# A hybrid decoder layer on one core: the gates' unit in two passes, rows of maxima laid by DMA, seam fills on another queue

## The chip, the cores and the metric

One core of a Trainium2 chip runs the whole layer in one launch. The metric is the device time of one execution in microseconds; the number given for a kernel is the median of three runs. A further execution was profiled, and all rows shown come from it.

## The reference

One layer, 2048 tokens of width 1024, float32. `proj = rmsnorm(x) @ w_in` feeds two groups of heads:

```python
q_ml, k_ml, v_ml, o_ml, gates        # mLSTM: 4 heads, chunkwise recurrence, gates = 8 columns of proj
c_q, c_kv, k_r = ...                 # MLA: 8 heads
q  = [rmsnorm(c_q) @ w_uq]           # 64 plain + 32 rotary columns a head
kv = [rmsnorm(c_kv) @ w_ukv]         # 64 key + 64 value columns a head
k  = concat(kv[..., :64], apply_rope(k_r, cos, sin))   # one rotary part (32) for all heads
p  = softmax(causal(q k^T / sqrt(96)));  h_mla = p v
x  = x + rmsnorm(concat(h_ml, h_mla) @ w_out)
x  = x + rmsnorm(relu(rmsnorm(x) @ w_up)^2 @ w_down)
```

The softmax needs the largest score of each query, or something near it, before `exp`.

## The kernel before

**Numbers.** Every float32 operand is split into a high part of type fp32r and the rest, and a product is three passes, high times high, high times rest, rest times high (`mm3`, L252 to 255: one line for each pass). The weights are split on the chip: ScalarE casts the high part (L464, L494), VectorE or GpSimd subtracts for the rest (L499). The rests are written to HBM (`wparts`) and loaded again for the later blocks of tokens (`wload`, L445), while the high part is made anew from the raw weights.

**Stages.** First come the input projections and the mLSTM, in four blocks of 512 tokens (0 to about 511 us). A block runs units of 128 columns, 8 k-tiles by 3 passes each: units 13 to 15 the latents, unit 0 a mixed one, 1 to 4 convolved q and k, 5 to 8 v, 9 to 12 the output gates, 16 to 18 the products behind the latents. The mixed unit 0 holds 8 gate columns, 56 of zeros, the 32 rotary key columns, and these again with their halves swapped. `stabiliser` (L962) scales its result into the tile `G`; `rotate` (L924) turns rows 64 to 95 with a table of sines in `trigd` and stores the turned keys in HBM (`krd`, L958 and L959).

Then comes attention (about 511 to 980 us): 8 heads by 4 query blocks of 512, called (h, qb). For each (h, qb) stand three kinds of work on TensorE: *maxima* `m` (L1594), which multiply high parts alone; scores `S` (L253 to 255, 3 passes); and products `o<-ph,V`, `o<-pl,V` and `o<-ph,onecol` (L1681, L1684, L1679). VectorE reduces each `m` to one column of `mp` (L1601, L1603), then all of a block to `mx`, 128 rows by 4 (L1622). To subtract a maximum from the scores, the operands have a 97th row: `K` has 1 there, `Q` the negative maximum. That row must lie along one partition, so TensorE turns `mx` by four matmuls with one column of weights each against the identity (`mt`, L1627), and ScalarE copies the 512 numbers, negated, from PSUM into row 96 of `QK` (L1630). The scores of (h, qb) wait for it. ScalarE takes two exponentials, VectorE or GpSimd subtracts them (`pl`, L1668). At the end of a (h, qb), `out_rows` (L1744) empties two accumulators: ScalarE copies 64 rows (`ot`, L1751), VectorE adds 64 (L1754) and copies the second accumulator (`ou`, L1758), GpSimd adds (L1761), and SP stores. The output projection and the MLP follow, to 2407 us; the change does not touch them.

**The seam.** At the end of the projections SBUF is handed over to attention in steps (`switch1` to `switch3`). Row 96 of `QK0` and `QK1` is filled from the input `edge` by three DMAs each, which GpSimd issues (`pool.dma_start`, L1496 and L1498); the fills of `V1` and `onecol` (L1492 to L1494) stand behind those of `QK1`. In the planner these six DMAs are put down as work of SP. SP issues all other loads: `krd` (L1540), `qkd` and `qrd` (L1546, L1548), values (L1561).

**What sets the order.** A planner (`Plan`, L130) gets every operation with its engine, a guessed duration, what it waits for, the buffers it takes and a key, runs them through in a time of its own, and writes each engine's instructions in the order found. Engines run that order strictly, each instruction waiting in place; SP does so with its DMAs too. GpSimd is POOL in the rows, VectorE DVE, ScalarE ACT, TensorE PE.

Of the kernel before, what the change touches and what calls it, by code (L numbers as in the profile page):

```python
# [10 lines left out]
F32 = mybir.dt.float32  # L11
# [43 lines left out]
OB = 1  # L55
QLO = 0
# [35 lines left out]
RB = (0, 0)  # L92
RK = (7, 7)
# [151 lines left out]
def trunk(ctx: ExitStack, tc: tile.TileContext, x, xT, pos, wu, wout, wup, wdn, cols, rows, consts, edge, out, dbg=None):  # L245
# [45 lines left out]
    qrd = dram.tile([2, P, 2, SEQ], F32, tag="qrd", name="qrd")  # L291
    krd = dram.tile([32, 2, SEQ], F32, tag="krd", name="krd")
# [24 lines left out]
    for name, bufs in (  # L317
        ("awr", WR), ("wh", 5), ("wl", 5), ("mma", 1), ("mmb", 1), ("pst", 1), ("chh", 1), ("sg", SG), ("cbc", 1), ("G", GB_), ("raw", 2), ("cy", 2), ("cth", 2),
# [27 lines left out]
    mrow = b1.tile([1, 20], F32, tag="mrow", name="mrow")  # L346
    cst8 = [b1.tile([P, 129], F32, tag=f"C{p}", name=f"C{p}") for p in range(2)]
# [39 lines left out]
    o_rest = pl.op("SP", 1000, load_rest, [o_fill], key=kA(0, 16), kb=70)  # L387

# [8 lines left out]
    o_fill2 = pl.op("Pool", 900, fills2, key=kA(0, -40))  # L397
    pl.op("Activation", 600, masks, [o_rest], key=kA(1, 0))
# [46 lines left out]
    def wload(b, u):  # L445
# [10 lines left out]
        def place_l():  # L456
            t["l"] = wp.tile([P, 1024], F32R, tag="wl", name=f"wl{b}_{u}", bufs=5)
# [14 lines left out]
        o_turn[:] = [gl]  # L472
# [4 lines left out]

    def wsplit(b, u):
        if b > STB[u]:
            return wload(b, u)  # L480
# [56 lines left out]
    def unit(b, u):  # L537
# [386 lines left out]
    def rotate(b, t, G):  # L924
# [4 lines left out]
        def load():  # L929
            t["tgr"] = e2.tile([P, TB], F32R, tag="cth", name=f"tg{b}")  # L930
            t["tg"] = f32(t["tgr"])
            dma(t["tg"][64:128], trigd[:, b * TB : (b + 1) * TB])
# [18 lines left out]
        g = pl.op("SP", 500, load, [o_rope[b % 2], G], key, take=("cth",), kb=128)  # L951
        o = pl.op(*cost, d1, [g, G], key)
# [9 lines left out]
    def stabiliser(b):  # L962
# [118 lines left out]
        h = pl.op("PE", 330, gates, [G, o_cst], key, take=("pst",), free=[("G", G)])  # L1081
# [1684 lines left out]
```

## Time and profile before

| | us |
|---|---|
| median of 3 runs | 2410.01 (2403.1 to 2412.87) |
| the profiled execution | 2408.7 |
| its span, first to last instruction | 2406.9 |
| TensorE busy, in the span | 2360.4 |
| VectorE, ScalarE, GpSimd busy | 1732.2, 1361.8, 815.3 |

How to read a row of a timeline: start in us, duration, engine, line, operation, what it writes and reads, count, and in brackets the idle time of its engine before it and what ended that. Successive matmuls overlap, so that a matmul's duration is longer than the step from its start to the next one's. DMA-issuing rows of SP and POOL show the issuing alone, not the transfer.

### The profile page before, as it was taken

The page shows a single profiled execution, that of the slowest core. Times are in us where ns is not written, and L with a number is a line of the kernel's source. Part 1 is how long each engine was busy: PE and PEld are TensorE (multiplying, and loading weights), DVE is VectorE, ACT ScalarE, POOL GpSimd, SP SyncE. Part 2 cuts the span into 40 slices and gives each one's busy share as a digit, 9 for nine tenths or more (in the row PEclk, how much of TensorE's full clock was granted, in tenths as well). Part 3 has the DMA queues.
Part 4 walks back from the last instruction along what each step waited for, and adds up shares of the span by engine and source line. Part 5 has one row for each costly group of instructions (what it writes and reads, how often), then busy time and mean ns, then how long its engine had stood idle before and what let it go on. Part 6 is the DMA issues. An engine that isn't in the chain of part 4 may idle for free. (4 is left out here: it accounts for less than half of the span.)

```text
span 2406.9 us, 34273 instructions
## 1 busy us (share of the span) xinstructions
PE 2360.4 (98%) x11141; PEld 1904.2 (79%) x11141; DVE 1732.2 (72%) x3105; ACT 1361.8 (57%) x2644; POOL 815.3 (34%) x698
## 2 busy tenths in 40 slices
PE   9999999989999999999999999999999999999997
PEld 7777878767777777788788888888888888888885
DVE  6867665658888888647767677766675677776777
ACT  5646454437778877444666556655564344433454
POOL 2725242538788888422000000000000223222346
PEclk9999999999999999999999999999999999999998
DMA  8697979886222321567777797665674445445358
GB/s 288 217 336 248 351 249 335 267 197 152 54 56 54 81 57 32 160 225 249 243 214 221 226 310 221 203 171 167 191 218 139 147 135 181 124 149 164 127 140 164
DMA packets 341308, 449.22 MB, mean 187 GB/s; under 512 B 34908, under 2 KB 227432, under 8 KB 341128
## 3 DMA queue, kind: packets, MB, share of 16 engines
q1 hardware_dynamic: 337192, 440.16, 58.7%
q0 software_dynamic: 3936, 6.87, 2.0%
q8 instruction: 88, 1.44, 0.3%
q14 instruction: 92, 0.75, 0.1%
HBM read 295.97 MB, written 153.05 MB: 187 GB/s over the span
## 5 line engine op out<-in xcount | busy, mean ns | idle before, releaser
L2575 POOL TENSOR_TENSOR y<-vd_0X,y 128x512 f32<-128x512 f32 x7 | 10.6, 1519 | 726.5 <-ACT vd_0X L2572 726.5
L1660 ACT ACTIVATE ph<-S 128x512 fp32r<-128x512 f32 (+1 forms) x320 | 170.3, 532 | 86.7 <-PE S L255 49.9
L1695 POOL TENSOR_TENSOR t<-t,ph 128x512 f32<-128x512 f32 (+1 forms) x192 | 212.9, 1109 | 17.3 <-ACT ph L1660 6.8
L2487 ACT CAST hh<-hr 128x512 fp32r<-128x512 f32 (+1 forms) x208 | 116.2, 567 | 157.0 <-PE d_5X L2538 15.4
L1668 DVE TENSOR_TENSOR pl<-S,ph 128x512 fp32r<-128x512 f32 (+3 forms) x271 | 156.4, 589 | 31.8 <-ACT S L1664 28.9
L253 PE MATMUL mm<-xh,wh 128*128 128x512 f32 x384 | 156.5, 408 | 4.2 <-DVE gate L1185 2.2
L2492 DVE TENSOR_TENSOR hl<-hr,hh 128x512 fp32r<-128x512 f32 (+1 forms) x208 | 133.0, 646 | 30.0 <-ACT hh L2487 23.5
L1601 DVE TENSOR_REDUCE mp<-m 128x1 f32<-128x512 f32 (+2 forms) x208 | 135.7, 666 | 25.2 <-PE m L1594 20.7
L254 PE MATMUL mm<-xl,wh 128*128 128x512 f32 x384 | 150.4, 392 | 0.8 <-DVE xl L424 0.8
L255 PE MATMUL mm<-xh,wl 128*128 128x512 f32 x384 | 150.3, 392 | 0.5 <-DVE wl L499 0.5
L1664 ACT ACTIVATE S<-S 128x512 f32<-128x512 f32 (+3 forms) x271 | 140.2, 517 | 0.4
L253 PE MATMUL S<-QK 97*128 97x512 f32 (+1 forms) x320 | 120.5, 377 | 2.1 <-DVE pl L1668 1.9
L1681 PE MATMUL o<-ph,V 128*128 128x512 f32 (+1 forms) x320 | 119.0, 378 | 1.8 <-DVE ot L1754 1.5
L1684 PE MATMUL o<-pl,V 128*65 128x512 f32 (+1 forms) x320 | 116.0, 363 | 3.4 <-POOL pl L1668 3.4
L1594 PE MATMUL m<-QK 96*128 96x512 f32 (+3 forms) x320 | 115.6, 388 | 1.8 <-DVE mp L1601 1.1
L254 PE MATMUL S<-QK 97*128 97x512 f32 (+1 forms) x320 | 116.9, 365 | 0.0
L255 PE MATMUL S<-QK 97*128 97x512 f32 (+1 forms) x320 | 116.7, 365 | 0.0
L253 PE MATMUL op<-wo,hh 128*128 128x512 f32 x256 | 100.9, 394 | 1.4 <-DVE osm L1985 1.0
L255 PE MATMUL op<-wo,hl 128*128 128x512 f32 x256 | 99.8, 390 | 0.0
L254 PE MATMUL op<-wo,hh 128*128 128x512 f32 x256 | 99.7, 389 | 0.0
L2326 ACT ACTIVATE t<-t 128x512 f32<-128x512 f32 x96 | 60.7, 632 | 65.0 <-DVE t L2321 64.6
L253 PEld LDWEIGHTS mm<-xh,wh 128*128 128x128 f32 x384 | 72.1, 188 | 22.8 <-DVE gate L1185 3.3
(6451 smaller groups left out, 7483.4 us busy)
## 6 DMA issues: line engine op xcount, KB each, us to landing
hr<-hd SPq DMA_DIRECT2D x100, 448.0 KB
wr<-in_wu_dram SPq DMA_DIRECT2D x71, 512.0 KB
hd<-t SPq DMA_DIRECT2D x128, 256.0 KB
hd<-ts SPq DMA_DIRECT2D x96, 256.0 KB
wl<-wparts SPq DMA_DIRECT2D x45, 512.0 KB
QK<-qkd SPq DMA_DIRECT2D x32, 512.0 KB
xt<-in_x_dram SPq DMA_DIRECT2D x28, 512.0 KB
xf<-xd SPq DMA_DIRECT2D x40, 256.0 KB
```

The costliest lines, as they stand in the source:

```text
L253: pe.matmul(o, ah, bh, start=start, stop=False)
L254: pe.matmul(o, ah, bl, start=False, stop=False)
L255: pe.matmul(o, al, bh, start=False, stop=stop)
L1601: vec.tensor_reduce(mp["t"][:, j, kb : kb + 1], ps[:, :n], axis=AX.X, op=ALU.max)
L1660: act.activation(t["h"][:, :w], t["S"][:, :w], AF.Exp)
L1664: act.activation(t["p"][:, :w], t["S"][:, :w], AF.Exp)
L1668: (pool if by_pool else vec).tensor_tensor(t["l"][:, :w], t["p"][:, :w], f32(t["h"][:, :w]), ALU.subtract)
L1681: pe.matmul(o0, v[:, 0:128], t["h"][:, :w], start=start, stop=stop)
L1684: pe.matmul(o1, v[:, 64:129], t["l"][:, :w], start=start, stop=stop)
L1695: pool.tensor_tensor(to, to, hv, ALU.add)
L2487: act.copy(t["h", m][:, :w], t["r", m][:, :w])
L2492: vec.tensor_tensor(t["l", m][:, :w], t["r", m][:, :w], f32(t["h", m][:, :w]), ALU.subtract)
```

## The change

Six things are changed.

1. **Unit 0 in two passes** (`wboth`). The rests of the 8 gate columns and of the 32 rotary columns are put into columns of the same tile that held zeros and the swapped copy. High and rest of the weights are then one operand, and unit 0 takes two passes a k-tile. The gates' high and rest are summed by the four small matmuls that turn them (`both8`, 16 rows in place of 8). Block 0 makes the tile and stores it; blocks 1 to 3 load it, 512 KB, with no raw weights and no cast.
2. **The rotary chain** (`rotate`) becomes longer for that: ScalarE copies the rest's 32 rows, an add joins them, and two DMAs inside SBUF make the swapped copy; the load of the sines stands behind the add.
3. **Rows of maxima of heads 1 to 7**: VectorE turns `mx` in 32x32 blocks (`mr`), and four DMAs inside SBUF, issued by SP, lay the 512 numbers into row 96. No matmul, no PSUM bank and no ScalarE copy is left there. Head 0 stays as it was. `K` has -1 in row 96 and `Q` the maximum.
4. **The second accumulator of heads 1 to 7** is copied by ScalarE in place of VectorE.
5. **At the seam**, the edge rows come from a copy of `edge` in HBM by DMAs on SP; GpSimd keeps the memsets, and `onecol` is filled ahead of `V1`. The scores wait for the edge rows, the maxima do not. The mask is loaded later, the rotary keys of `QK0` block by block, and the loads of head 1 wait for a given score step of head 0 each.
6. **Planner**: the second half of the sines is made from block 1 on, `out_rows` stores earlier by key, a weight's place waits for the cast of the one before, and some guessed durations are larger.

```diff
-RB = (0, 0)
-RK = (7, 7)
+RB = (0, 1)
+RK = (7, 0)
...
+    both8 = edger[0:16, 0:8]
+    o_both = pl.op("DVE", 70, lambda: vec.tensor_tensor(both8, ident[0:16, 0:8], ident[0:16, 8:16], ALU.add), [o_cst], key=kA(0, 10))
+    o_edge = pl.op("SP", 500, lambda: dma(edged, edge), key=kA(0, 30))
...
+    def wboth(b):
...
+        def lo():
+            h, r = (x.rearrange("p (k c) -> p k c", c=P) for x in (t["h"], t["r"]))
+            for m in (slice(8, 16), slice(96, 128)):
+                vec.tensor_tensor(h[:, :, m], r[:, :, m], f32(h[:, :, m]), ALU.subtract)
...
+        if b:
+            g = pl.op("X", 0, place, o_turn, kA(b, at - LLEAD), take=("wh",))
+            d = pl.op("SP", 500, lambda: dma(f32(t["h"]), wparts[0]), [g, *o_parts[0]], kA(b, at - LLEAD), kb=512)
...
+            if u == 0:
+                for i in range(2):
+                    pe.matmul(t["p"], w["h"][:, s], tiles[b, k][i], start=k + i == 0, stop=(k, i) == (KD - 1, 1))
+                return
             mm3(t["p"], w["h"][:, s], w["l"][:, s], *tiles[b, k], k == 0, k == KD - 1)
...
-                pe.transpose(t["p"][:, c * 8 : c * 8 + 8], t["G"][0:8, c * P : (c + 1) * P], ident[0:8, 0:8])
+                pe.matmul(t["p"][:, c * 8 : c * 8 + 8], t["G"][0:16, c * P : (c + 1) * P], both8, start=True, stop=True)
...
-        g = pl.op("SP", 500, load, [o_rope[b % 2], G], key, take=("cth",), kb=128)
-        o = pl.op(*cost, d1, [g, G], key)
+        g = pl.op("Activation", 570, move, [o_rope[b % 2], G], key, take=("cth",))
+        a = pl.op(*cost, add, [g], key)
+        w = pl.op("SP", 1000, swap, [a], key, kb=64)
+        l = pl.op("SP", 500, load, [o_rope[b % 2], a], key, kb=128)
+        o = pl.op(*cost, d1, [l, w], key)
...
-                pool.memset(f32(onecol[:, 0:64]), 0.0)
-                pool.memset(f32(onecol[:, 64:65]), 1.0)
             else:
-                pool.dma_start(Kh[s][96:97, :], edge[0:1])
+                dma(f32(Kh[s][96:97, :]), edged[0:1])
                 for z in (Kl, Ql):
-                    pool.dma_start(z[s][96:97, :], edge[1:2])
+                    dma(f32(z[s][96:97, :]), edged[1:2])
...
+        if h == 1:
+            war = [o_sc[(start_of[0, 1], start_of[0, 2], start_of[0, 2] + 6, start_of[0, 3])[b]]]
...
             vec.tensor_reduce(t["m"], mp["t"][:, :, 0 : qb + 1], axis=AX.X, op=ALU.max)
+            if h >= MROW:
+                t["r"] = a2.tile([P, 32], F32R, tag="mr", name=f"mr{h}_{qb}")
+                vec.transpose(f32(t["r"]), f32(pools["mx"][(h * NB + qb) % 2]))
...
+        def lay():
+            row = f32(Qh[s][96:97, qb * TB : (qb + 1) * TB]).rearrange("o (j b i) -> o b j i", b=4, i=32)
+            for i in range(4):
+                dma(row[:, i], f32(t["r"])[32 * i : 32 * i + 4])
...
+        if h >= MROW:
+            a = pl.op("DVE", 220, top_, [*reds, o_mx], key, take=("mr",), free=[("mp", mp["op"])])
+            o_m[h, qb] = pl.op("SP", 2200, lay, [a] + war, key, free=[("mr", a)], kb=4)
+            return
...
-            vec.tensor_copy(t["u"][0:65], acc_of[h, qb][1][0:65])
+            (act.copy if h >= MROW else vec.tensor_copy)(t["u"][0:65], acc_of[h, qb][1][0:65])
...
-        b = pl.op("SP", 1000, store, [a], key - 3, free=[("xr", o_ou)] if end else [("ot", o_ot), ("ou", o_ou)], kb=130)
+        b = pl.op("SP", 1000, store, [a], key - 60, free=[("xr", o_ou)] if end else [("ot", o_ot), ("ou", o_ou)], kb=130)
...
-    z = np.zeros((DM, 56), np.float32)
-    misc = np.concatenate([w[:, 1536:1544], z, kr, kr[:, 16:], kr[:, :16]], axis=1)
+    z = np.zeros((DM, 48), np.float32)
+    misc = np.concatenate([w[:, 1536:1544], w[:, 1536:1544], z, kr, kr], axis=1)
```

Three places in the engines' orders. First POOL at the first part of the seam, before: the last rows of unit 18 (`rs`), the edge DMAs of `QK0`, then two small steps of the mLSTM's chunks, `qs` and `sm`.

```order
L907 TENSOR_TENSOR rs_3_4735<-rt_1_4741,rs_3_4735 128x512 [waits DMAHW3_49,DMAHW2_49,Activation_49]
L1496 DMA QK_4791<-in_edge_dram 1x16x128 [waits DMAHW3_49,DMAHW2_49,DMAHW4_49,DMAHW1_49,DMAHW5_49,DMAHW0_49,DMAHW6_49,PE_49,Pool_49]
L1498 DMA QK_4791<-in_edge_dram 1x16x128 x2
L1235 TENSOR_TENSOR qs_1_4808<-qT_115,iwbc_1_4652 128x256 [waits DMAHW4_49,PE_49]
L1289 TENSOR_TENSOR sm_0_4805<-sm_0_4805,mhalf 128x4 [waits DVE_49]
```

The same place now:

```order
L953 TENSOR_TENSOR rs_3_4710<-rt_1_4716,rs_3_4710 128x512 [waits DMAHW3_49,DMAHW2_49,Activation_49]
L1550 MEMSET mx_4771 128x28
L1550 MEMSET mx_4772 128x28
L1294 TENSOR_TENSOR qs_1_4784<-qT_116,iwbc_1_4615 128x256 [waits DMAHW1_49,DMAHW0_49,PE_49]
L1348 TENSOR_TENSOR sm_0_4781<-sm_0_4781,mhalf 128x4 [waits DVE_49]
```

The DMAs, which wait for seven semaphores of transfers, are gone; two memsets without a wait stand there.

Second, POOL a little later, at the edge rows of `QK1` and the first `pl` of attention, before:

```order
L1289 TENSOR_TENSOR sm_3_5067<-sm_3_5067,mhalf 128x4 [waits DVE_49,Pool_49]
L1496 DMA QK_5188<-in_edge_dram 1x16x128 [waits DMAHW1_49,DVE_49,DMAHW6_49,Activation_49,Pool_49]
L1498 DMA QK_5188<-in_edge_dram 1x16x128 x2
L1492 MEMSET V_5186 128x64
L1493 MEMSET onecol 128x64
L1494 MEMSET onecol 128x1
L1668 TENSOR_TENSOR pl_0_0_5232<-p_0_0_5217,ph_0_0_5204 128x512 [waits Activation_49]
```

And now:

```order
L1348 TENSOR_TENSOR sm_3_5045<-sm_3_5045,mhalf 128x4 [waits DVE_49,Pool_49]
L1555 MEMSET onecol 128x64 [waits PE_49]
L1556 MEMSET onecol 128x1
L1563 MEMSET V_5164 128x64 [waits PE_49]
L1754 TENSOR_TENSOR pl_0_0_5209<-p_0_0_5195,ph_0_0_5182 128x512 [waits PE_49,Activation_49]
```

Here too no wait for a transfer is left ahead of `pl`.

Third, PE at the row of maxima of (1, 3), before; `S1_2` are scores of (1, 2), `o0_1_2` and `o1_1_2` its products, `m2_0` the maxima of (2, 0):

```order
L253 MATMUL S1_2_5_6345<-QK1_5188 128x512
L254 MATMUL S1_2_5_6345<-QK1_5188 128x512
L255 MATMUL S1_2_5_6345<-QK1_5188 128x512
L1627 MATMUL mt1_3_6353<-identr_63,mx1_3_6341 1x128 x4
L1681 MATMUL o0_1_2_6307<-ph1_2_11_6300,V0_5102 128x128
L1684 MATMUL o1_1_2_6308<-pl1_2_11_6317,V0_5102 65x128
L1594 MATMUL m2_0_3_0_6365<-QK0_4791 128x512
```

Now that row is laid by SP, among the stores of finished rows (`hT`, `sumd`, `recd`, `rsm`) and loads of the next heads:

```order
L1861 DMA recd_76<-rsm0_3_6147 128x4
L1855 DMA rsm1_0_6242<-sumd_75 128x4
L1620 DMA QK1_5166<-qrd_66 16x2x512
L1712 DMA QK1_5166<-mr1_3_6236 1x4x32 x4
L1635 DMA V1_5164<-vd_69 128x4x128
L1851 DMA sumd_75<-ou1_1_6287 1x512
```

The four matmuls have left PE, and four DMAs stand on SP behind others that wait for their own data. On PE, 79 rows stand between the last maxima of (1, 3) and its first score in the new order, 48 of them with 512 columns; for (5, 3) it is 70 rows and 41, the fewest of any (h, qb) of heads 1 to 7.

More of the change, by code (lines that the diff above doesn't have):

```diff
@@ L55 @@
 OB = 1
+WL = 5
+VONE = 40.0
+MKEY = -45.0
+MROW = 1
+CKEY = -100.0
 QLO = 0
@@ L476, in wload, with start, hi, place @@
         return t
+    def wboth(b):
+        t = {}
+        at = TIME[b][0]
+        def start():
+            t["r"] = wp.tile([P, 1024], F32, tag="wr", name=f"wr{b}_0", bufs=WR)
+        def hi():
+            t["h"] = wp.tile([P, 1024], F32R, tag="wh", name=f"wh{b}_0", bufs=5)
+            act.copy(t["h"], t["r"])
+        def lo():
+            h, r = (x.rearrange("p (k c) -> p k c", c=P) for x in (t["h"], t["r"]))
+            for m in (slice(8, 16), slice(96, 128)):
+                vec.tensor_tensor(h[:, :, m], r[:, :, m], f32(h[:, :, m]), ALU.subtract)
+        def place():
+            t["h"] = wp.tile([P, 1024], F32R, tag="wh", name=f"wh{b}_0", bufs=5)
+        if b:
+            g = pl.op("X", 0, place, o_turn, kA(b, at - LLEAD), take=("wh",))
+            d = pl.op("SP", 500, lambda: dma(f32(t["h"]), wparts[0]), [g, *o_parts[0]], kA(b, at - LLEAD), kb=512)
+        else:
+            a0 = pl.op("X", 0, start, key=kA(b, at - WLEAD), take=("awr",))
+            a = pl.op("SP", 500, lambda: dma(t["r"], wu[0]), [a0], key=kA(b, at - WLEAD), kb=512)
+            g = pl.op("Activation", 963, hi, [a], kA(b, at - SPLIT0), take=("wh",))
+            d = pl.op("DVE", 600, lo, [g], kA(b, at - SPLIT0), free=[("awr", a0)])
+            o_parts[0] = [pl.op("SP", 500, lambda: dma(wparts[0], f32(t["h"])), [d], kA(b, at + WSTORE), free=[("wh", g)], kb=512)]
+        t["op"], t["free"] = [d] * KD, [("wh", g)]
+        return t
     def wsplit(b, u):
+        if u == 0:
+            return wboth(b)
         if b > STB[u]:
@@ L927, in rotate, with move, add, swap @@
         s = slice(64, 96)
-        def load():
+        def move():
             t["tgr"] = e2.tile([P, TB], F32R, tag="cth", name=f"tg{b}")
             t["tg"] = f32(t["tgr"])
+            act.copy(t["tg"][s], t["G"][96:128])
+        def add():
+            eng.tensor_tensor(t["G"][s], t["G"][s], t["tg"][s], ALU.add)
+        def swap():
+            dma(t["G"][96:112], t["G"][80:96])
+            dma(t["G"][112:128], t["G"][64:80])
+        def load():
             dma(t["tg"][64:128], trigd[:, b * TB : (b + 1) * TB])
@@ L1080, in stabiliser @@
         rotate(b, t, G)
-        h = pl.op("PE", 330, gates, [G, o_cst], key, take=("pst",), free=[("G", G)])
+        h = pl.op("PE", 330, gates, [G, o_both], key, take=("pst",), free=[("G", G)])
         o = pl.op("DVE", 590, g1, [h, o_rest], key, free=[("pst", h)])
@@ L1452, in switch1 @@
         pq = pp(pc, "pq", 1)
+        pools["mx"] = [a1.tile([P, 32], F32R, tag=f"mx{i}", name=f"mx{i}") for i in range(2)]
     def switch2():
@@ L1567, in load_v @@
             after = [o_s2, o_const["v0"], *([o_sc[start_of[0, qb - 2]]] if qb > 1 else o_last if qb else [])]
-        o_v[g, t] = [pl.op("SP", 1000, load, [o_vd[t], o_vd[t + 1], *after], key, kb=660)]
+        o_v[g, t] = [pl.op("SP", 1300, load, [o_vd[t], o_vd[t + 1], *after], key, kb=660)]
     def maxima(h, qb, keys):
@@ L1778, in out_rows @@
         z = pl.op("DVE", 680, add0, [o_ot], key - 3, free=[("o0", o_first)])
-        o_ou = pl.op("DVE", 680, copy1, [o_end], key - 3, take=("xr" if end else "ou",), free=[("o1", o_first)])
+        o_ou = pl.op(*(("Activation", 585) if h >= MROW else ("DVE", 680)), copy1, [o_end], key - 3, take=("xr" if end else "ou",), free=[("o1", o_first)])
         if end:
```

51 lines of the change are left out of this document (32 added, 19 removed).

## The prediction

> **What bounds the kernel now.** I read the page's busy times, then the waits of TensorE, then the timelines around its two longest stalls ahead of the tail.
>
> ```profile
> span 2406.9 us, 34273 instructions
> PE 2360.4 (98%) x11141; PEld 1904.2 (79%) x11141; DVE 1732.2 (72%) x3105; ACT 1361.8 (57%) x2644; POOL 815.3 (34%) x698
> ```
>
> TensorE is busy for 98% of the span; what leaves its queue is gained, wherever it would otherwise be at work. How much one matmul is worth must not be read from its duration, since matmuls overlap. In a stretch of the MLP where TensorE never idles, nearly all matmuls have 512 columns:
>
> ```profile
> 1600.00:1700.00 100.00, 100.00 (x443) 82.81 (x442) 68.60 (x108) 61.24 (x108) 0.00 (x0) 1.00 0.60 177
> L255 PE MATMUL mm<-xh,wl 128*128 128x512 f32 x384 | 150.3, 392 | 0.5 <-DVE wl L499 0.5
> ```
>
> 443 matmuls in 100 us are 0.226 us each, against a mean duration of 392 ns in the second row. I count 0.226.
>
> The whole idle time of TensorE is 46.5 us (span less busy). The longest waits, from the view of waits, are these (engine and line, what it waited for, total, times, longest):
>
> ```profile
> PE o L1684 <- POOL pl L1668: 3.4, 3, 3.0
> PE num L1241 <- DVE hn L1295: 3.0, 1, 3.0
> ```
>
> Both stand at the seam. The earlier one, by engine:
>
> ```profile
> 481.06 0.66 PE L1265 MATMUL kv<-vext,kw 128*64 128x129 f32 x8
> 484.75 1.61 PE L1241 MATMUL num<-vext,E 128*128 128x129 f32 x8 [3.04 <-DVE hn L1295]
> 477.39 0.16 DVE L1285 SCALAR_TENSOR_TENSOR sm<-sm 128x4 f32<-128x4 f32 x1 [0.58 <-ACT jk L1279]
> 483.94 0.76 DVE L1295 TENSOR_TENSOR hn<-num,sm 128x256 f32<-128x256 f32 x2 [3.75 <-POOL sm L1289]
> 480.44 0.75 POOL L1496 DMA_DIRECT2D QK<-in_edge_dram  x1 [6.32 <-DMA maskneg<-in_consts_dram]
> 481.19 1.00 POOL L1498 DMA_DIRECT2D QK<-in_edge_dram  x2
> 482.87 1.04 POOL L1289 TENSOR_TENSOR sm<-sm,mhalf 128x4 f32<-128x4 f32 x1
> ```
>
> VectorE has its part of `sm` ready at 477.55. GpSimd needs 1.04 us for its own, but starts at 482.87: it has stood 6.32 us at the edge DMA in front of it, issued three, and run a `qs`. VectorE's `hn` follows, which frees the accumulator that TensorE needs. The later one:
>
> ```profile
> 520.98 0.40 PE L1681 MATMUL o<-ph,V 128*128 128x512 f32 x1
> 524.35 0.69 PE L1684 MATMUL o<-pl,V 128*65 128x512 f32 x1 [2.97 <-POOL pl L1668]
> 518.03 0.59 ACT L1664 ACTIVATE p<-S 128x512 f32<-128x512 f32 x1
> 521.25 0.59 POOL L1496 DMA_DIRECT2D QK<-in_edge_dram  x1 [10.71 <-DVE mp L1601]
> 521.83 0.97 POOL L1498 DMA_DIRECT2D QK<-in_edge_dram  x2
> 523.02 1.27 POOL L1668 TENSOR_TENSOR pl<-p,ph 128x512 fp32r<-128x512 f32 x1
> ```
>
> The data of `pl` are there at 518.62; GpSimd reaches it at 523.02, behind the other edge DMAs. The granted clock is the third number from the right in the next view:
>
> ```profile
> 484.00:490.00 6.00, 5.25 (x25) 4.33 (x26) 1.63 (x6) 1.59 (x9) 0.73 (x1) 0.72 0.81 200
> 524.00:530.00 6.00, 5.65 (x22) 4.44 (x23) 2.10 (x4) 1.17 (x2) 0.30 (x1) 0.53 1.12 199
> ```
>
> After each stall TensorE ran at a reduced clock for some time: 6 x (1 - 0.72) = 1.7 us lost, and 6 x (1 - 0.53) = 2.8 us.
>
> **The change part by part.**
>
> *Unit 0.* One pass of three goes: 8 a block, 4 blocks, 32 matmuls x 0.226 = **7.2 us** off TensorE. In blocks 1 to 3 a cast and one of two 512 KB loads go as well; both lie beside TensorE's work and I count nothing. If a startup wait of block 0 swallows its part, 1.8 us are lost again.
>
> *Rows of maxima.* The four `mt` matmuls, with their neighbours on TensorE:
>
> ```profile
> 606.67 0.40 PE L255 MATMUL S<-QK 97*128 97x512 f32 x1
> 606.90 0.40 PE L1627 MATMUL mt<-identr,mx 128*1 128x128 f32 x4
> 607.14 0.27 PE L1681 MATMUL o<-ph,V 128*128 128x128 f32 x1
> ```
>
> 607.14 - 606.90 = 0.24 us a row, 28 rows: **6.7 us** off TensorE. In exchange each row takes this way, from the same block (1, 3); the row of `recd` gives the shortest, median and longest time of issuing one such small DMA in ns:
>
> ```profile
> 599.82 0.40 PE L1594 MATMUL m<-QK 96*128 96x512 f32 x1
> 605.34 0.15 DVE L1622 TENSOR_REDUCE mx<-mp 128x4 fp32r<-128x16 f32 x1
> 613.79 0.40 PE L253 MATMUL S<-QK 97*128 97x512 f32 x1
> L1775 SPq DMA_DIRECT2D recd<-rsm x32: 319/334/712, 551.9 to 999.2; - x32
> 644.81 0.39 SPq L1765 DMA_DIRECT2D sumd<-ou  x1
> 646.91 0.34 SPq L1769 DMA_DIRECT2D rsm<-sumd  x1
> ```
>
> From the last maxima matmul to the end of `mx` it takes 5.7 us, as VectorE comes to it late. The transpose isn't in the trace; between the 0.15 of `mx` and the 0.68 of a full-width VectorE step I take 0.2, nearest to the small one. Four issues at 0.33 make 1.3 us. `rsm` is issued once `sumd` has landed, 2.1 us after that one's issue began. Together 5.7 + 0.2 + 1.3 + 2.1 = 9.3 us. In the new order 48 matmuls of 512 columns and 31 shorter rows stand between for (1, 3), some 48 x 0.226 + 31 x 0.11 = 14.3 us (a 256-column matmul is half of 0.226); for (5, 3), the tightest, 41 and 29 give 12.5. So the rows should land 3 to 5 us ahead of need, if SP is free. That cover is what the slow rival attacks.
>
> *Edge rows.* With GpSimd rid of them, `sm` can start at 477.55 and the first stall goes: 3.0 + 1.7. TensorE reaches `num` at about 481.7, `sm` and `hn` end at about 477.6 + 1.0 + 0.8 = 479.4. Of the second, memsets of 0.5 us at most and `pl` of 1.27 follow 518.62, which ends at 520.4 or earlier, against TensorE's arrival at 521.2: 3.0 + 2.8 (0.2 of it counted twice). Together **10.3 us**. SP issues the six now, and stands at the place where its `krd` loads for `QK1` stood before with the same waits; behind them are value loads. Bounds of this term: nothing, if SP's transfers then come late; 10.3.
>
> The Trainium skill, page "DMA: Bandwidth & Descriptors", section "Issuing engines are not separate DMA queues", says that DMAs of all issuing engines run on the same 16 engines and that another issuer saves only the sequencer's issue time. By that rule this term would be the 0.75 + 1.00 + 0.59 + 0.97 = 3.3 us of issuing on GpSimd; the rows show that the wait in front of the issue, 6.32 and 10.71 us, is what TensorE paid for. Its page "TensorE: Matmul & The Clock Gate", section "What's actually happening", has the clock halved after at least one idle window of about 3.4 us; taken strictly, idle times of 3.04 and 2.97 would cost no clock, and the term would be 6.0. Here the granted clock fell after both.
>
> *Second accumulator.* From the groups by line:
>
> ```profile
> L1758 DVE COPY ou<-o 65x512 f32<-65x512 f32 x32 | 21.8, 682 | 8.4 <-PE o L1684 5.2 <-issue 2.0 <-POOL t L1692 1.0
> L1630 ACT ACTIVATE QK<-mt 1x512 fp32r<-1x512 f32 x32 | 18.7, 586 | 10.8 <-PE mt L1627 9.9
> ```
>
> 28 x 0.68 = 19 us leave VectorE, 28 transposes come. ScalarE loses 28 copies of 0.59 and takes 28 of about the same, so its load in attention stays. TensorE's waits for VectorE there are short; between a loss of 2 (two ScalarE copies in a row ahead of the next exponential) and a gain of 3 I take 0.
>
> *Rotary chain.* Longer by a ScalarE copy, an add and a transfer inside SBUF:
>
> ```profile
> L959 SPq DMA_DIRECT2D krd<-G x4: 313/318/1077, 110.3 to 443.2; - x4
> L1540 SPq DMA_DIRECT2D QK<-krd x8: 557/590/640, 479.8 to 522.7; - x8
> ```
>
> The last turned keys leave at 443.2 and are first read at 479.8. The extra chain is some 0.6 + 0.7 + 1 + 2.1 = 4.4 us (the copy like `L1630`, the add like a VectorE step, two issues, one landing): hidden by 36 us. Its swap waits in SP's queue for the add, with weight loads behind; nothing counted, up to 3 us lost if VectorE is late.
>
> *Seam loads and planner.* They reorder the projections in every block. TensorE idles 46.5 - 6.0 us apart from the two stalls, and a new order can gain or lose some of that; I take 0, with 6 us either way.
>
> Sum: 7.2 + 6.7 + 10.3 = 24.2 us. The profiled execution took 2408.7 us, 1.8 above its span and 1.3 under the median of the runs, 2410.0. So 2408.7 - 24.2 = 2384.5, or about **2386 us** as a median.
>
> **The rivals.**
>
> *A, the stalls only move (0.20).* The matmuls go, 13.9 us, but SP, which carries everything at the seam, now makes TensorE wait for a value or key load, at best sparing GpSimd's 3.3 us of issuing: 2410.0 - 13.9 = 2396, or 2393. For it: transfers take a share of 1.12 of the engines' time in the row of 524 to 530. Against it: no wait of TensorE for a transfer appears among its waits before. This is where the Trainium skill's rule on issuing engines would land.
>
> *B, the new order is also better (0.13).* VectorE's 19 us and the lighter projections remove 6 to 10 us more of TensorE's 40 remaining: 2376 to 2380.
>
> *C, the rows land late (0.09), on the other side.* SP issues in order, and in front of the four DMAs stand stores that wait for others:
>
> ```profile
> SPq L1764 <- POOL ot L1761: 73.8, 28, 6.5
> SPq L1765 <- DVE ou L1758: 84.2, 21, 11.9
> ```
>
> The mean waits are 2.6 and 4.0 us, inside the cover of 3 to 5; the longest are outside. A row that comes 3 us late stalls TensorE for 3 and, like the two stalls above, costs about 2 us of clock: 5 us. With 3 late rows the result is 2401, with 5 the gain is gone, and with all 28 rows delayed by 2 us on average, 56 us less 24.2, it is 2442. It decides against the change from about 5 late rows on.
>
> **How the numbers follow.** The forecast has 0.58, with 2379 to 2394 as its own range. The range for 8 in 10 takes in B and A with their 6 us of order: 2374 to 2400. A measurement of this kernel can tell about 0.5%, 12 us, from no change, so faster means under 2398, slower over 2422. Faster: forecast 0.58, B 0.13, A's lower part 0.06, together 0.77. Within: the rest of A 0.14 and a mild C of 0.02, 0.16. Slower: 0.07.
>
> **What would show it.** Right: TensorE's stalls of 3.0 us at the seam and the reduced clock there are gone; 32 fewer `mm` and 112 fewer `mt` matmuls; attention is shorter by some 7 us, the projections by 7. Wrong: TensorE waiting for a DMA into `QK` ahead of scores of (h, 3) (C), or for values at the start of attention (A), or more idle time in the projections than before.

## The result

The changed kernel takes 2391.1 us (median of 6 runs, 2389.8 to 2396.6) against 2408.7 us of the kernel before (6 runs, 2403.1 to 2412.9): a ratio of 0.9930, 95% interval 0.9919 to 0.9941, some 17 us less. A second group of five runs gave 2394.2 against 2410.7, 0.9933 (0.9920 to 0.9946). The forecast was 2386, 24 us less. The profiled execution is the longest of its six runs, 2396.6 us, 12.1 less than that of before; stage by stage these two give:

| us, profiled executions | before | after |
|---|---|---|
| first to last `mm` (projections) | 503.3 | 503.3 |
| first to last `S` (attention) | 462.1 | 446.9 |
| last `S` to the last matmul | 1413.9 | 1416.3 |
| span | 2406.9 | 2394.8 |

Attention gained 15.2 us, more than forecast. The projections gained nothing, although 32 matmuls have left them and the stall at 481 us is gone. The last row grew by 2.4 us in a stage that the change does not touch; most of that is a half clock of 6.83 us in place of 3.41, behind the same wait of 3.0 us for `y`. TensorE between the first and the last `mm`, before and after (the length, then TensorE's busy time):

```profile
6.99:510.33 503.34, 489.84 (x2517) 389.21 (x2517) 330.48 (x678) 256.67 (x509) 204.64 (x180) 1.00 0.83 283
7.95:511.23 503.28, 488.72 (x2501) 385.95 (x2501) 335.55 (x683) 254.94 (x510) 200.89 (x180) 0.99 0.82 279
```

Its idle time there went from 13.5 to 14.6 us, the wrong way, and its busy time fell by 1.1 us only, where 32 matmuls would be 7.2. A part of that is one more half clock, in which TensorE is busy for longer with the same work (below). Another is the four small matmuls that turn the gates, here with the next matmul behind them, before (two rows) and after:

```profile
38.09 0.41 PE L976 MATMUL gp<-cst,G 8*128 8x8 f32 x4
38.43 0.50 PE L253 MATMUL mm<-xh,wh 128*128 128x512 f32 x1
38.29 1.05 PE L1035 MATMUL gp<-edger,G 16*128 16x8 f32 x8
39.27 0.50 PE L258 MATMUL mm<-xh,wh 128*128 128x512 f32 x1
```

They are eight instructions a block now, and take 0.98 us of TensorE's row in place of 0.34. In four blocks that is 2.6 us, for which the prediction counted nothing. The busy times from the page, and the longest waits of TensorE:

```profile
PE 2350.6 (98%) x11013; PEld 1895.6 (79%) x11013; DVE 1722.4 (72%) x3110; ACT 1357.2 (57%) x2645; POOL 812.0 (34%) x695
```

```profile
PE mm L258 <- DVE gate L1244: 4.4, 2, 3.6
PE d_7X L2623 <- DVE y L2646: 3.0, 1, 3.0
PE kt L1311 <- DVE C L1327: 2.8, 1, 2.8
```

The page has 128 matmuls fewer than before: 32 of unit 0 and 112 of the rows of maxima, less the 16 more of `gp`. The wait at `d_7X` lies in the MLP and was as long before. The two waits at the seam are no longer among the longest, but two others are, at `gate` and at `C`, which the kernel before did not have at that length. The windows, the two of the seam first (third number from the right: the granted clock):

```profile
484.00:490.00 6.00, 5.39 (x40) 4.17 (x39) 2.14 (x8) 1.85 (x5) 0.00 (x0) 1.00 0.71 152
524.00:530.00 6.00, 6.00 (x34) 4.52 (x33) 5.78 (x12) 4.76 (x11) 2.66 (x3) 1.00 0.79 209
210.00:216.00 6.00, 5.72 (x24) 4.14 (x25) 2.33 (x8) 3.79 (x14) 3.40 (x3) 0.72 0.57 141
443.00:449.00 6.00, 5.47 (x16) 4.06 (x17) 3.61 (x6) 1.22 (x2) 2.83 (x3) 0.72 0.54 193
```

At the seam the clock is full now; behind the new waits it is 0.72, a loss of 6 x 0.28 = 1.7 us each. So 2.8 + 1.7 + 3.6 + 1.7 = 9.8 us have appeared in the projections. The first place, block 1, by engine:

```profile
200.83 0.59 SPq L988 DMA_DIRECT2D tg<-trigd  x1
204.53 2.84 DVE L993 TENSOR_TENSOR G<-G,tg 32x512 f32<-32x512 f32 x1 [1.80 <-DMA tg<-trigd]
207.41 1.10 DVE L996 TENSOR_TENSOR tg<-G,tg 32x512 f32<-32x512 f32 x1
208.54 0.68 DVE L999 TENSOR_TENSOR G<-G,tg 32x512 f32<-32x512 f32 x1
209.53 0.60 DVE L1327 SCALAR_TENSOR_TENSOR C<-C,sp,kv 128x129 f32<-128x129 f32 x2
204.46 2.37 POOL L541 TENSOR_TENSOR wl<-wr,wh 128x1024 fp32r<-128x1024 f32 x1 [4.16 <-ACT wh L536]
210.28 0.41 PE L1311 MATMUL kt<-cst,kT 128*128 128x128 f32 x2 [2.81 <-DVE C L1327]
```

VectorE first stands 1.80 us for the sines of the rotary chain, then spends 4.6 us on three steps for which the planner had put down 0.69 each, and only then comes to the state update `C` that TensorE waits for. The steps are stretched: the first takes 2.84 us while GpSimd runs `wl`, the last 0.68 with GpSimd quiet. That the steps stand so late here has to do with item 6 too. The table of sines for blocks 1 and 3 is the last to be stored (stores before, then after; their first and last start stand behind the durations):

```profile
L1392 SPq DMA_DIRECT2D trigd<-kk x4: 469/532/1308, 80.5 to 118.3; - x4
L1451 SPq DMA_DIRECT2D trigd<-kk x4: 491/555/596, 78.2 to 192.0; - x4
```

In the kernel before it was stored at 118 us, and the steps of block 1 were done at 195.9 us; now it is stored at 192 us. No version makes it early again, so what this alone does to block 1 stays open. The second place, block 3:

```profile
436.06 1.67 DVE L993 TENSOR_TENSOR G<-G,tg 32x512 f32<-32x512 f32 x1
437.76 1.67 DVE L996 TENSOR_TENSOR tg<-G,tg 32x512 f32<-32x512 f32 x1
439.46 1.65 DVE L999 TENSOR_TENSOR G<-G,tg 32x512 f32<-32x512 f32 x1
441.79 0.95 DVE L1005 TENSOR_TENSOR G<-G,tg 32x512 fp32r<-32x512 f32 x1 [0.68 <-ACT tg L1002]
442.77 0.69 DVE L1244 TENSOR_TENSOR gate<-mm,rsbc 128x512 f32<-128x512 f32 x1
437.14 1.73 POOL L833 TENSOR_TENSOR ks<-ks 128x512 fp32r<-128x512 f32 x1
443.52 0.75 PE L258 MATMUL mm<-xh,wh 128*128 128x512 f32 x1 [3.57 <-DVE gate L1244]
```

Four steps in a row keep VectorE for 6.7 us ahead of the `gate` that empties TensorE's accumulator. In attention, the new rows went much as forecast (time of an issue in ns, shortest/median/longest):

```profile
L1712 SPq DMA_DIRECT2D QK<-mr x112: 572/573/865, 551.9 to 926.2; - x112
```

The transpose takes 0.21 us (estimated 0.2), an issue 0.573 (taken as 0.33). No wait of TensorE for a row is in its list.

### The profile page after: what moved, and what is told of

Same layout as the page of the kernel before. It is cut to its first block, busy times and chain, and to the rows that moved or that the text cites. A ratio compares the mean times of both kernels' runs of the same rounds, so it can differ in the third digit from the quotient of the medians.

```text
span 2394.8 us, 34280 instructions
## 1 busy us (share of the span) xinstructions
PE 2350.6 (98%) x11013; PEld 1895.6 (79%) x11013; DVE 1722.4 (72%) x3110; ACT 1357.2 (57%) x2645; POOL 812.0 (34%) x695
## 4 chain that ended last, share of the span: by engine, by line
PE 54%; DVE 2%; DMA 1%; issue 0%; ACT 0%; POOL 0%; DVEq 0%; SPq 0%; ACTq 0%; POOLq 0%
PE op L258 1%; PE op L260 1%; PE op L259 1%; PE d_4X L2623 1%; PE d_2X L2625 1%; PE d_4X L2625 1%; PE d_3X L2625 1%; PE d_3X L2624 1%; PE d_2X L2624 1%; PE d_4X L2624 1%; PE d_3X L2623 1%; PE d_2X L2623 1%; PE d_5X L2624 1%; PE d_5X L2623 1%; PE d_6X L2623 1%; PE d_1X L2625 1%
## 5 line engine op out<-in xcount | busy, mean ns | idle before, releaser
L1781 POOL TENSOR_TENSOR t<-t,ph 128x512 f32<-128x512 f32 (+1 forms) x192 | 213.2, 1110 | 15.2 <-ACT ph L1746 4.2
L258 PE MATMUL mm<-xh,wh 128*128 128x512 f32 x352 | 144.0, 409 | 5.3 <-DVE gate L1244 4.4
L259 PE MATMUL mm<-xl,wh 128*128 128x512 f32 x352 | 138.3, 393 | 1.4 <-DVE xl L433 1.3
L260 PE MATMUL mm<-xh,wl 128*128 128x512 f32 x352 | 138.3, 393 | 0.5 <-DVE wl L541 0.5
L1668 PE MATMUL m<-QK 96*128 96x512 f32 (+3 forms) x320 | 110.7, 385 | 2.5 <-DVE mp L1675 1.1
L258 PEld LDWEIGHTS mm<-xh,wh 128*128 128x128 f32 x352 | 66.3, 188 | 22.7 <-DVE gate L1244 5.2
```

The costliest lines, as they stand in the source:

```text
L258: pe.matmul(o, ah, bh, start=start, stop=False)
L259: pe.matmul(o, ah, bl, start=False, stop=False)
L260: pe.matmul(o, al, bh, start=False, stop=stop)
L1781: pool.tensor_tensor(to, to, hv, ALU.add)
```

## The experiments

The theory after the two traces: the rotary steps, where they now stand in VectorE's row, take back some 10 us of the gain. Its rivals: the stalls were an accident of one execution; the projections are bound by something else in the new order; any new order shifts stalls about. A second question was what each part is worth. Times are compared as ratios to the kernel before, measured in the same group; one 0.001 is 2.4 us, and each interval is about 0.0013 to either side. The changed kernel stands at 0.99315, the mean of its two, so that a difference from it is known to about 4 us. A single profiled execution tells more of a stage than of the whole: what follows the last `S`, which no version edits, took between 1411 and 1419 us in the 14 profiles.

### The changed kernel again

No edit.

> The changed kernel once more, beside the others of this group. Theory (the longer rotary chain on VectorE makes TensorE wait in blocks 1 and 3 of the projections): the profile shows both stalls again, near 210 us (2.8 us idle) and near 443 us (3.6 us idle), each with the granted clock at half behind it, and the last mm starts near 511 us. Rival (the stalls were an accident of one execution): at least one of them is gone and the projections end up to 5 us earlier; the one execution profiled so far was the slowest of six, 2396.6 against a median of 2391.1. Time by both: 2390 to 2396 us.

Measured: 0.9933. Both stalls are there again, 209.65 and 443.50 us, each with the half clock, and the last `mm` starts at 511.22. That of block 3 is no accident: it is also in the profiles of the five versions below that keep VectorE's order in the projections (a third pass, edge rows by GpSimd, the second accumulator by VectorE, rows by TensorE, and these two together), always 3.57 or 3.58 us. That of block 1 comes and goes: 2.8 us in two of these five, 1.0 to 1.1 us without a half clock in the other three, where VectorE stands 0.3 to 0.6 us for the sines and not 1.8 or more. In the one with the second accumulator by VectorE:

```profile
202.99 0.68 DVE L993 TENSOR_TENSOR G<-G,tg 32x512 f32<-32x512 f32 x1 [0.32 <-DMA tg<-trigd]
208.38 0.41 PE L1311 MATMUL kt<-cst,kT 128*128 128x128 f32 x2 [0.96 <-DVE C L1327]
```

### Without three rotary steps

```diff
 def d1():
+    if b:
+        return
     eng.tensor_tensor(t["G"][s], t["G"][s], t["tg"][s], ALU.mult)
 # d2 and d3 likewise
```

> The changed kernel with three of VectorE's rotary steps (the two products and the sum) left out in blocks 1 to 3, so that the keys of those blocks are stored unturned; the copy, the add, the swap, the cast and the rest stay, and each engine's order is otherwise the same. Theory (these steps hold the state update of block 1 and the gate of block 3 back): both stalls and the half clock behind them go, 2.8 + 1.7 + 3.6 + 1.7 = 9.8 us, so about 2381 us, and the last mm starts near 501 to 503 us. Rival (the projections are bound by something else in the new order, and VectorE's lateness is only the last wait to be seen): within 3 us of the changed kernel, 2388 or more.

Measured: 2390.1 us, 0.9911 (0.9897 to 0.9925), 4.9 us less than the changed kernel. The clock stays full through the projections, and the last `mm` starts at 507.05, 4.2 earlier: half of what the theory asked. Block 3 by engine:

```profile
435.65 0.69 DVE L1250 TENSOR_TENSOR gate<-mm,rsbc 128x512 f32<-128x512 f32 x1
441.80 0.69 DVE L881 COPY vs<-vp 128x512 f32<-128x512 f32 x1 [1.70 <-DMA qkd<-ks]
440.49 0.34 SPq L914 DMA_DIRECT2D tb<-trep  x1
440.88 3.89 SPq L857 DMA_DIRECT2D qkd<-ks  x4
443.17 0.50 PE L258 MATMUL vp<-wh,ch 128*128 128x512 f32 x1 [2.04 <-ACT vs L878]
```

The `gate` comes 7.1 us earlier. But SP stands until 440.49 at a load that reads back a table just stored, the stores of `ks` are queued behind it, VectorE's `vs` waits for the buffer that they free, ScalarE's `vs` behind that, and TensorE 2.04 us for it. So the steps did cause the stall of block 3, and, with the wait for the sines in front of them, that of block 1 where it occurs; and in block 3 a wait of SP was hidden under theirs, which is next.

### The planner told what a step takes

```diff
-eng, cost = ... (vec, ("DVE", 690))
+eng, cost = ... (vec, ("DVE", 1700))
```

> The changed kernel with the planner told that a rotary step on VectorE takes 1700 ns in place of 690, nothing else. In its order the steps of blocks 1 and 3 no longer stand in one row: in block 3 the gate comes after two of them and not after four, in block 1 the state update after one and not after three. Theory (the row of steps is what TensorE waits for): 5 to 10 us less than the changed kernel, 2381 to 2386 us, neither stall above 2 us. Rival (a new order is a lottery): other stalls take their place, within 3 us of it or slower.

Measured: 2386.1 us, 0.9902 (0.9889 to 0.9915); 7.1 us less than the changed kernel. VectorE's rows in blocks 1 and 3:

```profile
203.21 0.69 DVE L993 TENSOR_TENSOR G<-G,tg 32x512 f32<-32x512 f32 x1
206.37 0.61 DVE L1327 SCALAR_TENSOR_TENSOR C<-C,sp,kv 128x129 f32<-128x129 f32 x2 [0.68 <-PE kv L1324]
208.62 2.69 DVE L996 TENSOR_TENSOR tg<-G,tg 32x512 f32<-32x512 f32 x1
...
432.80 0.69 DVE L996 TENSOR_TENSOR tg<-G,tg 32x512 f32<-32x512 f32 x1
433.93 0.69 DVE L1244 TENSOR_TENSOR gate<-mm,rsbc 128x512 f32<-128x512 f32 x1 [0.44 <-PE mm L260]
435.84 1.19 DVE L999 TENSOR_TENSOR G<-G,tg 32x512 f32<-32x512 f32 x1
```

`C` and `gate` now wait for TensorE, not TensorE for them; between the steps stands other work. The last `mm` starts at 502.92, 8.3 earlier; TensorE's idle time between the first and the last `mm` is 9.4 us in place of 14.6, and no half clock is left before the end of the MLP. This version beats both kernels. Its order differs in more than the rotary steps, on TensorE and GpSimd too, so that not all of the gain need be theirs.

### The rotary steps on GpSimd

```diff
-KPOOL = (0,)
+KPOOL = (0, 1, 2, 3)
-... (pool, ("Pool", 1350)) if b in KPOOL ...
+... (pool, ("Pool", 2100)) if b in KPOOL ...
```

> The changed kernel with the rotary steps of all four blocks on GpSimd (told to the planner at 2100 ns each), none on VectorE. Theory (what TensorE waits for is the row of rotary steps on VectorE): both stalls under 1.5 us and no half clock in the projections, 2384 to 2388 us, like the version whose planner spreads them. Rival (GpSimd is then late with the rests of the latents and keys): TensorE waits for GpSimd instead, 2391 us or more.

Measured: 2396.5 us, 0.9944 (0.9932 to 0.9956), 3 us more than the changed kernel and so the same within the error. Both stalls are gone (the longest wait of TensorE in the projections is below 2 us), yet the last `mm` starts at 509.57, only 1.7 earlier. In their place stand waits of 1.0 to 1.3 us, for VectorE's `wl` and `vs` and a load of `QK`, and a half clock of 3.4 us at 219.6; the idle time is 13.9 us, hardly less. The theory fails here: with the stalls away the gain did not come. That rules out reading 9.8 us as the value of the two stalls under any order; which of the smaller waits GpSimd's load brings about was not separated.

### Unit 0 in three passes with the short chain

The joined weights, the two passes, `both8` and the longer `rotate` are undone; the rest of the change stays.

```diff
 def wsplit(b, u):
-    if u == 0:
-        return wboth(b)
...
-g = pl.op("Activation", 570, move, [o_rope[b % 2], G], key, take=("cth",))
-a = pl.op(*cost, add, [g], key)
-w = pl.op("SP", 1000, swap, [a], key, kb=64)
-l = pl.op("SP", 500, load, [o_rope[b % 2], a], key, kb=128)
+g = pl.op("SP", 500, load, [o_rope[b % 2], G], key, take=("cth",), kb=128)
```

> The changed kernel with the merge of unit 0 and its longer rotary chain undone, three passes and the short chain, the rest of the change kept. Theory (32 matmuls gain 7.2 us, and the longer chain's place in VectorE's row loses some 8 of them again): 2390 to 2396 us, the same as the changed kernel within 3 us; the stall near 443 us is under 2 us. Rival (the merge is worth its 7 us in full and the stalls belong to the new order of the rest): 7 us slower, with both stalls still there.

Measured: 2398.2 us, 0.9955 (0.9942 to 0.9968), 5.7 us more than the changed kernel: the theory's "the same within 3 us" fails, and the result is near the rival's 7. The stall of block 3 is gone, that of block 1 is longer, 4.4 us; VectorE's row there:

```profile
210.16 0.68 DVE L976 TENSOR_TENSOR G<-G,tg 32x512 f32<-32x512 f32 x1 [5.60 <-DMA tg<-trigd]
211.60 0.68 DVE L982 TENSOR_TENSOR G<-G,tg 32x512 f32<-32x512 f32 x1
212.96 0.60 DVE L1307 SCALAR_TENSOR_TENSOR C<-C,sp,kv 128x129 f32<-128x129 f32 x2
```

With the short chain too, the planner puts three steps ahead of `C` (two are shown), and VectorE stands 5.60 us for the sines, which are stored at 192 us here as well. So the longer chain is not needed for the stall in block 1; the place in VectorE's row and the late sines are enough. What the merge is worth follows only in part: in the profiled execution (2401.2 us) the projections are 2.6 us longer, with the same idle time and one half clock less (1.7 us), so that TensorE has 4.3 us more to do there. Attention is 3.8 us longer with a half clock of 10.24 us from 520.6 us, in which TensorE never idles; why it came is open, and the merge does not explain it.

### A third pass again

```diff
-for i in range(2):
-    pe.matmul(..., tiles[b, k][i], ..., stop=(k, i) == (KD - 1, 1))
+for i in range(3):
+    pe.matmul(..., tiles[b, k][i % 2], ..., stop=(k, i) == (KD - 1, 2))
```

> The changed kernel with a third pass in unit 0 again, of the same high parts once more, so that the unit's result is false; 32 matmuls more on TensorE, each engine's order otherwise the same. If 32 matmuls are worth 32 x 0.226 as forecast: 7 us slower than the changed kernel, 2398 us, with the last mm near 518 us. Rival (the projections got no shorter because unit 0's matmuls lay beside waits): at most 3 us slower.

Measured: 2400.1 us, 0.9957 (0.9944 to 0.9971), 6.1 us more. From first to last `mm` it takes 507.5 us, 4.2 more than the changed kernel. In this execution the stall of block 1 is 1.1 us and leaves the clock alone, while a wait of 1.9 us at 491 us has a half clock with it. In all, TensorE idles 12.3 us there against 14.6, and both executions have two half clocks of 3.41 us. So the third pass takes 4.2 + 2.3 = 6.5 us, against 7.2 forecast. The eight small matmuls a block stay as they are in this run.

### Edge rows by GpSimd again

```diff
-dma(f32(Kh[s][96:97, :]), edged[0:1])
+pool.dma_start(Kh[s][96:97, :], edge[0:1])
# Kl and Ql likewise
```

> The changed kernel with the six edge DMAs issued by GpSimd again, at the planner's places for them, the rest of each engine's order the same. In the new order only a ScalarE-fed product stands behind the first three (the next of GpSimd's work there waits for a transfer until 490.7 us anyway), but the part of pl that starts at 519.6 us stands behind the last three, which cannot be issued before 521.5 us. Theory (a wait in front of an issue blocks what stands behind it): the stall of some 3 us near 523 us comes back with 2.8 us of clock behind it, 5 to 6 us slower than the changed kernel. Rival (another issuer saves its issuing alone): 6 issues of 0.25 to 0.35 us on SP against some 0.6 on GpSimd, at most 2 us slower. A stall near 485 us as well would make 10 us.

Measured: 2398.4 us, 0.9952 (0.9939 to 0.9964), 4.9 us more. GpSimd and TensorE at the place of the second stall:

```profile
521.40 0.58 POOL L1565 DMA_DIRECT2D QK<-in_edge_dram  x1 [10.62 <-ACT S L1750]
523.17 1.28 POOL L1754 TENSOR_TENSOR pl<-p,ph 128x512 fp32r<-128x512 f32 x1
524.50 0.69 PE L1770 MATMUL o<-pl,V 128*65 128x512 f32 x1 [2.88 <-POOL pl L1754]
```

The stall is back as it was in the kernel before, and in the profile attention is 5.5 us longer while the projections are the same (503.5 us). The first stall is not back: in the new order GpSimd does its `sm` at 481.88 us, ahead of the first three DMAs at 482.86.

### The kernel before, edge rows alone

```diff
-pool.dma_start(Kh[s][96:97, :], edge[0:1])
+dma(f32(Kh[s][96:97, :]), edged[0:1])
# Kl and Ql likewise; o_edge copies edge to HBM in block 0
```

> The kernel before with this part alone: a copy of the edge rows in HBM and the six DMAs issued by SP, the order otherwise the same. Theory: both stalls at the seam and the half clock behind them go, 10.3 us, about 2398 us beside 2408.7. Rival one (issuing alone): 3.3 us, 2405. Rival two (SP takes over the wait and holds its loads back, so that TensorE waits for those): no gain, 2405 to 2412, with a wait of TensorE for a DMA into QK or V near 520 us.

Measured: 2412.1 us, 1.0004 (0.9995 to 1.0012): nothing. Both stalls of before are gone; in their place, SP and TensorE, and the same for attention (the last two rows):

```profile
481.55 2.53 SPq L1542 DMA_DIRECT2D QK<-krd  x4
484.76 1.25 SPq L1550 DMA_DIRECT2D QK<-qrd  x2
490.62 0.30 PE L1596 MATMUL m<-QK 96*128 96x128 f32 x1 [3.68 <-DMA iwbc<-wd]
547.13 0.69 DVE L1760 COPY ou<-o 65x512 f32<-65x512 f32 x1 [3.51 <-DMA sumd<-ou]
548.47 0.50 PE L253 MATMUL S<-QK 97*128 97x512 f32 x1 [3.22 <-DVE pl L1670]
```

TensorE comes to the first maxima of head 0 earlier than before, and their loads are not there. (The name in the bracket is the transfer that landed last by the profile; the maxima read `QK`.) Attention starts without its stall too, but 25 us later VectorE stands 3.51 us for the store that frees `ou`: SP issues it at 541.43 us, behind loads, and not earlier than before (540.48). TensorE then waits 3.22 us, with a half clock of 3.41 us. So both gains are lost at the next thing that SP has to bring. The rival of moving stalls holds here. The change has the stores earlier by key (item 6), but no version tests that alone.

### The kernel before, the whole of item 5

Item 5 of the change, on the kernel before; its core:

```diff
-o_mask = pl.op(..., key=EKEY - 30, kb=256)
+o_mask = pl.op(..., key=MKEY, kb=256)
-rotary_keys(s, b, -40 if s else EKEY - 30 + b)
+rotary_keys(s, b, -40 if s else keys[0, b, "m"][0] - LDK - 2)
-a = pl.op("PE", ..., mm, [o_q[h, qb][0], o_k[h, kb][0], o_kr[s, kb], o_const[s]], key, ...)
+a = pl.op("PE", ..., mm, [o_q[h, qb][0], o_k[h, kb][0], o_kr[s, kb]], key, ...)
```

> The kernel before with the whole of item 5: the edge rows on SP as in the run with the edge rows alone, which gained nothing since TensorE then waited 3.7 us for the keys and queries of head 0 at 490.6 us, and besides the mask loaded later, the rotary keys of QK0 loaded block by block behind the head's other loads, maxima that don't wait for edge rows, and the fills and waits of head 1. Theory (the order of SP's seam loads decides whether the removed wait is a gain): the wait at 490 us shrinks to under 1 us and the two old stalls stay away, 8 to 10 us faster than before. Rival (the seam's stalls only change their place whatever the order): within 4 us of before.

Measured: 2408.6 us, 0.9996 (0.9987 to 1.0004): nothing again. TensorE at the first maxima, with the load that they follow, and at a new place in attention:

```profile
480.91 0.61 SPq L1551 DMA_DIRECT2D QK<-krd  x1
487.91 0.44 PE L1607 MATMUL m<-QK 96*128 96x128 f32 x1 [3.35 <-DMA QK<-qrd]
824.39 0.93 PE L1607 MATMUL m<-QK 96*128 96x512 f32 x2 [1.59 <-DVE mp L1614]
```

My theory fails: the better order of loads is not enough. The first stall (4.7 us) has become a wait of 3.35 us for the loads of head 0 with 1.7 us of clock. The second is gone, but a wait of 1.59 us at 824 us is followed by the half clock (0.72 over the 6 us from 487 and from 824), and attention as a whole is 1.5 us shorter. In the changed kernel the way from the first `krd` load to the first maxima is as long, 7 us, but TensorE arrives with it (0.61 us of waiting), and in the version with the spread steps without any. Why the new order brings SP to that load sooner, relative to TensorE, was not taken apart.

### The second accumulator by VectorE again

```diff
-(act.copy if h >= MROW else vec.tensor_copy)(t["u"][0:65], ...)
+vec.tensor_copy(t["u"][0:65], ...)
```

> The changed kernel with the second accumulator of heads 1 to 7 copied by VectorE again, at the same places, all else in the same order. Counted at nothing in the prediction. Attention became 15.2 us shorter, of which the rows of maxima explain 6.7 and the second stall 5.7; theory: the 2.8 us left are VectorE's relief by these 28 copies, so 2 to 3 us slower than the changed kernel. Rival: they lie beside other work on either engine, within 1 us.

Measured: 2399.4 us, 0.9950 (0.9937 to 0.9962), 4.5 us more. Attention is 8.4 us longer in its profile, of which 4 are idle time of TensorE and 1.7 a half clock at 644 us; the projections are 2.6 us shorter, as the stall of block 1 is only 1.0 us in this execution. Two of TensorE's waits in attention (515 to 985 us):

```profile
PE o L1767 <- DVE ot L1840: 3.8, 10, 0.9
PE S L258 <- DVE pl L1754: 2.4, 6, 0.7
```

In the changed kernel these are 0.3 us, once, and 0.8, twice. The first product of the next block waits for the accumulators, and with VectorE doing two of the three steps that empty them, TensorE arrives first.

### Rows of maxima by TensorE again, and both

```diff
-MROW = 1
+MROW = 8
# and, for the rows alone, copy1 by ScalarE from head 1 on
```

> The changed kernel with the rows of maxima of all heads made by TensorE's matmuls and ScalarE's copy from PSUM again, while ScalarE still copies the second accumulators. With both undone the loss was about 10 us, with the accumulator alone undone about 5. If the row matmuls are worth 28 x 0.24 us: 7 us slower than the changed kernel; if ScalarE's two copies a block then hinder its exponentials, up to 10. Rival (the accumulator was all of it): under 3 us slower.

> The changed kernel with both the rows of maxima and the second accumulator of heads 1 to 7 made as before: 112 one-column matmuls and 28 ScalarE copies from PSUM again, no transposes and no row DMAs. If the rows are worth 28 x 0.24 us and the accumulator 2 to 3: 9 to 10 us slower than the changed kernel, of which 6.7 are TensorE's matmuls. Rival (the row matmuls lay beside waits): under 4 us slower. The projections should end where they do in the changed kernel, near 511 us.

Measured: the rows alone 2399.8 us, 0.9962 (0.9949 to 0.9974), 7.4 us more than the changed kernel; both together 2405.4 us, 0.9972 (0.9963 to 0.9982), 9.8 more. In the profile of the first, the `mt` matmuls take 6.7 us more of TensorE's row in attention than in the changed kernel (31 rows in place of 3, from their start to the next matmul), which is what they were counted at. That the 7.4 us are so near is luck in part: attention is 10.0 us longer, 1.4 of it matmuls of the output projection that stand earlier, and the projections are 3.5 us shorter, as the stall of block 1 is small there. The accumulator adds 2.4 us to the rows, which is inside the error, or 4.5 where it alone is undone.

## Why the prediction came out as it did

The kernel became faster, by two thirds of what the sum gave. Two terms of the sum were too large, one was too small, and one was missing. That the time still lies near the forecast is luck in part, since the stages do not: by the terms the projections should have gained 7.2 + 4.7 = 11.9 us and attention 12.3; they gained 0 and 15.2. More idle time in the projections than before, one of the prediction's own signs of being wrong, is what came.

**Unit 0, 7.2 us: too large.** The matmuls were counted nearly right: a third pass costs 6.1 us by the medians and 6.5 by the profile. But the sum put at nothing what the gates' four small matmuls take more on TensorE, 2.6 us, so that some 4 are left; the version with three passes has 4.3 more of TensorE's work in the projections.

**Rows of maxima, 6.7 us: right.** 6.7 by TensorE's row, 7.4 by the medians. Their cover of 3 to 5 us sufficed, though the four issues took 2.3 us and not 1.3; the slow rival did not occur.

**Edge rows, 10.3 us: half.** Of the second stall the reading was right in the changed kernel: with GpSimd issuing again it comes back, 4.9 us by the medians and 5.5 by the profile. In the kernel before its gain was lost again, at a store on SP. The Trainium skill's page "DMA: Bandwidth & Descriptors", section "Issuing engines are not separate DMA queues", says that issuing DMAs on several engines saves only the time of issuing. Taken for a move from one engine to another, that would be 3.3 us in all; it leaves out what decides here, the wait in front of an issue that holds up the work behind it (10.62 us). For the first stall, the step "with GpSimd rid of them, `sm` can start at 477.55 and the first stall goes" is true, and the clause after it, "TensorE reaches `num` at about 481.7", was followed no further: in the kernel before it then runs into loads that land at 487 to 490 us, and the 4.7 us are gone again. I had named that as rival A and given it 0.20. In the changed kernel the first stall is away whether SP or GpSimd issues; it is owed to the new order, not to the queue.

**Second accumulator, 0: too small.** 2.4 to 4.5 us by the medians, and more by attention in the one profile (8.4). The step "TensorE's waits for VectorE there are short" was read from the total; what the copy relieves is one short wait at the start of many blocks.

**Rotary chain, 0, and seam loads and planner, 0 with 6 either way: the step that failed.** "Hidden by 36 us" asked when the turned keys are read, not what stands behind the steps in VectorE's row. "Up to 3 us lost if VectorE is late" priced the transfer, not the steps, and 0.7 us stood for one where 0.68 to 2.84 is measured. Where the planner put them costs up to 7.1 us, as the version with the spread steps shows, and 4.9 by the version without three of them; with all of them on GpSimd nothing was gained. In block 1 this does not need the longer chain, and the sines that item 6 stores later bear on it, which was not tested alone.

By undoing, the parts are worth 5.7 (merge with its chain) + 9.8 (rows and accumulator) + 4.9 (edge rows) = 20.4 us, against 16.5 for all together (0.00685 x 2410). Each of the three is known to about 4 us, and the 4 us between are no more than that; parts that meet in one order don't add up exactly. With the spread steps the gain is 0.0098 x 2410 = 23.6 us, near the 24.2 of the forecast, but not for its reasons: terms that were off make up for each other.

## What to carry to other kernels

Before counting a longer chain as hidden, list for each of its steps what stands behind it in its engine's row and who waits for that, and price the step at what it takes beside the neighbours that it will have. Where a planner sets the order, a guess of 0.69 us for a step that takes up to 2.84 can cost more than the step itself; correct the guess first. When matmuls are taken out, count the small ones that are put in: here they cost 2.6 of 7.2 us. When a stall goes, follow the engine to its next operand: a stall's length, with the half clock behind it, is an upper bound of the gain, and in the kernel before the whole of both was lost, to the next load and to the next store.

## What the runs showed of the hardware

VectorE's step on 32x512 elements took 0.68 us with GpSimd quiet, 1.67 beside GpSimd's steps on 128x512, which themselves took up to 1.73 there and 1.29 elsewhere, and 2.84 beside one on 128x1024. The Trainium skill's page "GPSIMD Engine Reference", section "1. Specifications", says that the two engines share their way into SBUF and contend where a VectorE instruction has two inputs in SBUF, as these steps do; the rows agree.

The granted clock fell to half for 3.41 us after idle times of 2.81 and 3.57 us, and in the kernel before with item 5 after one of 1.59 us; after one of 2.04, where the rotary steps were left out, it stayed full. The half clocks of one execution start whole multiples of 3.413 us apart (in the changed kernel at 211.48, 443.59 and 2368.70 us, 68 and 564 of them). Laid on such a grid, the wait of 2.04 us falls on two of its windows, 1.2 and 0.8 us, while the one of 1.59 lies in a single window that has 1.9 us of idle time in all. In the 14 profiles, between the start-up and the end of the MLP, each window with 1.8 us or more was followed by the half clock; of those with 1.0 to 1.6 us some were and most were not. The Trainium skill's page "TensorE: Matmul & The Clock Gate", section "What's actually happening", speaks of one idle window of about 3.4 us, with windows that run freely. Ahead of the end of the program the half clock lasted 3.41 us or a multiple of it, which agrees; but by these rows a wait shorter than a window can do, and where it falls in the windows matters beside its length.
